# Layer 1's query operands: two transposes per token tile instead of four, the swapped operand copied in SBUF

## The chip, the cores and the metric

The kernel runs on one core of one Trainium2 chip. The metric is the device time of one execution in microseconds (us); lower is better. A core has five engines that run on their own and meet at semaphores: TensorE (PE in the profile, its weight loads PEld), VectorE (DVE), ScalarE (ACT), GpSimd (POOL) and SyncE (SP), which issues the DMAs. Each engine works through its own queue strictly in order. TensorE writes to PSUM, the other engines read PSUM and SBUF.

## The reference

Two layers of a diffusion backbone over 512 latent tokens and 256 context tokens, model width 1024, float32. Layer 0 is a windowed and a dense attention side by side, layer 1 a differential attention; each layer is followed by a SwiGLU network. The change is in layer 1's attention:

```python
q = _rms(q.reshape(b, n, HEADS_C, 2, d), qn)      # 8 heads, 2 halves of 64
k = _rms(k.reshape(b, n, HEADS_C, 2, d), kn)
if use_rope:
    q, k = _rope(q, cos, sin), _rope(k, cos, sin)
...
s = jnp.einsum('bqhad,bkhad->bhaqk', qb, k).astype(jnp.float32) * scale
p = jax.nn.softmax(s, axis=-1)
a = (p[:, :, 0] - lam * p[:, :, 1]).astype(v.dtype)
return jnp.einsum('bhqk,bkhe->bqhe', a, v)
```

Queries come from the 512 latent tokens alone, keys and values from all 768 tokens.

## The kernel before

A float32 product is made of rounded parts. A value v is split into a high part hi (v cast to float32r) and a low part lo = v - hi, and TensorE multiplies the parts. For the scores of layer 1 the parts lie above each other on the partitions: head size is 64, so a stack of two parts fills 128. The key operand `kT[:, a]` holds, for half a, the high part of the keys in partitions 0 to 63 and the low part in 64 to 127. The query operand `qt[:, j, a]` holds one part twice: j = 0 the high part above the high part, j = 1 the low part above the low part. Two matmuls into the same bank (L715 and L716) add up hi·hi + hi·lo and lo·hi + lo·lo.

**Work per head.** Layer 1 has 8 heads, each with six token tiles of 128: two of context (4, 5), then four latent (0 to 3), in the order of `CTX_FIRST`. For each tile `project` sums the input projection in one PSUM bank (`inps`, L465; 24 matmuls, in two halves with other work between). `Proj1.finish` then copies the sums to SBUF on ScalarE (`qkv`, L677), which frees the bank for the next tile; GpSimd copies the values (`vv`, L678); ScalarE squares, VectorE sums the squares (L422) and applies weights and rotation (L427 to L433), GpSimd makes the reciprocal root (`rs_q`, L159, L160) and scales (`qy`, L680). Then the parts are made: `qd` high on ScalarE (L685), `qd` low on VectorE (L686), `kd` high on ScalarE (L688), `kd` low on GpSimd (L689). Some steps later the closure `transposes` turns them on TensorE (`qpt`, L696, four transposes of 128x128 for a latent tile; `kpt`, L702, two) and ScalarE copies the results to SBUF (`qt`, L698; `kT`, L703).

**Attention.** `attend1` handles one tile of 128 queries of one head: eight score matmuls (`sc`, L715, L716, for two halves a), for each half a maximum on VectorE (`mx`, L718) and an exponential on ScalarE (`e`, L720); VectorE combines the halves (`rc`, `rt`, `e`, L723 to L727); TensorE transposes the result (`ppt`, L734), ScalarE and VectorE copy it out (`PT`, L739 and L737), TensorE multiplies with the values (`av`, L744); ScalarE scales (`o`, L746, L749), GpSimd makes a root (`rs_o`), VectorE normalises (`o`, L751).

**How they are woven.** The main loop runs over i, the 32 pairs of head and query tile. One pass issues the scores of i, three steps of the next heads' projection (a step is half a token tile), the transposes and value products of i - 1, and whichever `transposes` closures are due: a closure becomes due five steps after its tile was summed. So a head's projection runs while the head before is attended, and twelve steps make a period of one head. Weights of the next head (`weight1`) are loaded in four units by SyncE, cast on ScalarE (`wih`, L370) and subtracted on GpSimd (`wil`, L371); there are five buffers for them and two for the raw loads.

The order of instructions on each engine is made by the tile framework's scheduler, from dependences and its own estimate of durations. It is fixed at build time, so a change of one instruction can reorder others.

Of the kernel before, what the change touches and what calls it, by code (L numbers as in the profile page):

```python
# [12 lines left out]
F32R = mybir.dt.float32r  # L13
# [6 lines left out]
P = 128  # L20
# [7 lines left out]
HD = 64  # L28
# [23 lines left out]
def bc(ap, pos, n):  # L52

    dims = [list(d) for d in ap.ap]
    return AP(ap.tensor, ap.offset, dims[:pos] + [[0, n]] + dims[pos:])
# [8 lines left out]
def backbone(es: ExitStack, tc: tile.TileContext, x, c, ctx, c_ctx, mod_w, mod_b, norm_mix_w, norm_ffn_w,  # L64
# [3 lines left out]
    nc = tc.nc  # L68
# [33 lines left out]
    def tr_tile(name, shape, dt=F32, one=None):  # L102
        if one is None:
            one = turn["tr"] = 1 - turn["tr"]
        return p_1.tile(shape, dt, name=name, tag=f"tr{one}")
# [10 lines left out]
    def f32(ap):  # L116
        return ap.bitcast(F32)
# [13 lines left out]
    identr = cp.tile([P, P], F32R, name="identr")  # L131
# [248 lines left out]
    def rope_tables(pool, wq, wk):  # L380

        rp = raw_tile([P, NTX, 2, HD], "rp")
        nc.sync.dma_start(rp, rope)
        w = pool.tile([P, 2, HD], F32, name="rw", tag="rw")
        nc.sync.dma_start(w[:, 0, :], dram_rows(wq))
        nc.sync.dma_start(w[:, 1, :], dram_rows(wk))
        nc.vector.tensor_scalar(w[:, 0, :], w[:, 0, :], HD ** -0.5, None, ALU.mult)
        tb = pool.tile([P, 2, NTX, 2, HD], F32, name="rt", tag="rt")
        for j in range(2):
            nc.vector.tensor_tensor(tb[:, j, :, 0, :], rp[:, :, 0, :], bc(w[:, j, :], 1, NTX), ALU.mult)  # L390
            sw = swap_pairs(w[:, j, :])
            nc.vector.tensor_tensor(tb[:, j, :, 1, :].rearrange("p t (a b) -> p t a b", b=2),
                                    rp[:, :, 1, :].rearrange("p t (a b) -> p t a b", b=2),
                                    bc(sw, 1, NTX), ALU.mult)
        return w, tb
# [21 lines left out]
    def rotate_all(raw, h0, n, t, wc, tb, pool):  # L417

        sq = pool.tile([P, n * HD], F32, name="sq", tag="qz", bufs=2)
        nc.scalar.activation(sq, raw, AF.Square)  # L420
        ss = small.tile([P, n], F32, name="qss", tag="qss")
        nc.vector.tensor_reduce(ss, sq.rearrange("p (h d) -> p h d", d=HD), AX.X, ALU.add)  # L422
        r = rsqrt(ss, n, 1.0 / HD, "q")
        y = pool.tile([P, n, HD], F32, name="qy", tag="qy", bufs=2)
        rh = raw.rearrange("p (h d) -> p h d", d=HD)
        if t >= NTX:
            nc.vector.tensor_tensor(y, rh, wc[:, h0:h0 + n], ALU.mult)  # L427
            return y, r
        z = pool.tile([P, n, HD], F32, name="qz", tag="qz", bufs=2)
        nc.vector.tensor_tensor(z.rearrange("p h (a b) -> p (h a) b", b=2),  # L430
                                swap_pairs(raw), tb[:, t, 1].rearrange("p h (a b) -> p (h a) b", b=2), ALU.mult)
        nc.vector.tensor_tensor(y, rh, tb[:, t, 0], ALU.mult)
        nc.vector.tensor_add(y, y, z)  # L433
        return y, r
# [46 lines left out]
    def weights0(b, wp, subs, new_tile=raw_tile, loads=((0, 1), (), (2,), (3,))):  # L481
# [3 lines left out]
        for u in range(4):  # L485
# [13 lines left out]
            subs[u % len(subs)].tensor_sub(lo, raw, f32(hi))  # L499
            yield hi, lo  # L500

    def tables0(j, tabs, wp):
        tabs[j] = rope_tables(wp, *((ev_qn_a[0], ev_kn_a[0]) if j == 0 else (ev_qn_b[0], ev_kn_b[0])))

# [152 lines left out]
    class Proj1:  # L657
# [14 lines left out]
        def finish(self, t, ps):  # L672

            n, wp, kT, qs = self.width(t), self.wp.pool, self.kT, self.qs
            m, h0 = (n - P) // HD, 0 if t < NTX else 2
            raw = wp.tile([P, 384], F32, name="qkv", tag="qkv", bufs=4)
            nc.scalar.copy(raw[:, :n], ps[:, :n])  # L677
            nc.gpsimd.tensor_copy(self.vv[:, t, :], raw[:, n - P:n])  # L678
            y, r = rotate_all(raw[:, :n - P], h0, m, t, self.wc, self.tb, wp)
            nc.gpsimd.tensor_tensor(y, y, bc(r, 2, HD), ALU.mult)  # L680
            nq = m - 2
            if nq:
                qd = wp.tile([P, 2, 2, 2, HD], F32R, name="qd", tag="qd", bufs=3)
                yb = bc(y[:, 0:2], 2, 2)
                nc.scalar.copy(qd[:, 0], yb)  # L685
                nc.vector.tensor_sub(qd[:, 1], yb, f32(qd[:, 0]))  # L686
            kd = wp.tile([P, 2, 2, HD], F32R, name="kd", tag="kd", bufs=3)
            nc.scalar.copy(kd[:, :, 0, :], y[:, nq:nq + 2])  # L688
            nc.gpsimd.tensor_sub(kd[:, :, 1, :], y[:, nq:nq + 2], f32(kd[:, :, 0, :]))  # L689

            def transposes():
                if nq:
                    pt = tr_tile("qpt", [P, 2, 2, P], F32R)
                    for j in range(2):
                        for a in range(2):
                            nc.tensor.transpose(pt[:, j, a, :], qd[:, j, a].rearrange("p a d -> p (a d)"), identr)  # L696
                    qt = self.qp.tile([P, 2, 2, P], F32R, name="qt", tag="qt", bufs=5)
                    nc.scalar.copy(qt, f32(pt))  # L698
                    qs[t] = qt
                pk = tr_tile("kpt", [P, 2, P], F32R)  # L700
                for a in range(2):
                    nc.tensor.transpose(pk[:, a, :], kd[:, a].rearrange("p a d -> p (a d)"), identr)  # L702
                nc.scalar.copy(kT[:, :, t * P:(t + 1) * P], f32(pk))  # L703
            return transposes

    def attend1(h, t, state, o_t, nlam, subln, mp):
        qs, kT, vv = state.qs, state.kT, state.vv
        mx = small.tile([P, 2], F32, name="mx", tag="mx")
        sm = small.tile([P, 2], F32, name="sm", tag="sm")
        E = []  # L710
        for a in range(2):
            sc = p_sc.pool.tile([P, 1024], F32, name="sc", tag="sc", bufs=2)
            for s0, k0, k1 in ((256, SEQ, TOK), (512, 0, SEQ)):
                so = sc[:, s0:s0 + k1 - k0]
                nc.tensor.matmul(so, qs[t][:, 0, a, :], kT[:, a, k0:k1], start=True, stop=False)  # L715
                nc.tensor.matmul(so, qs[t][:, 1, a, :], kT[:, a, k0:k1], start=False, stop=True)  # L716
            s = sc[:, 256:256 + TOK]
            nc.vector.tensor_reduce(mx[:, a:a + 1], s, AX.X, ALU.max, negate=True)  # L718
            e = mp.tile([P, TOK], F32, name="e", tag="e", bufs=PBUF)
            turn["exp"] = nc.scalar.activation(e, s, AF.Exp, bias=mx[:, a:a + 1], accum_out=sm[:, a:a + 1])  # L720
            E.append(e)
        rc = small.tile([P, 2], F32, name="rc", tag="rc")
        nc.vector.reciprocal(rc, sm)  # L723

        rt = small.tile([P, 1], F32, name="rt", tag="rt")
        nc.vector.scalar_tensor_tensor(rt, sm[:, 0:1], nlam, rc[:, 1:2], ALU.mult, ALU.mult)
        nc.vector.scalar_tensor_tensor(E[0], E[1], rt, E[0], ALU.mult, ALU.add)  # L727
        yield
        vt = [4, 5, 0, 1, 2, 3]
        pts = []  # L730
        for g0, m in ((0, 4), (4, 2)):
            pt = tr_tile("ppt", [P, 4, P])
            for a in range(m):
                nc.tensor.transpose(pt[:, a, :], E[0][:, (g0 + a) * P:(g0 + a + 1) * P], ident)  # L734
            PT = mp.tile([P, 4, P], F32, name="PT", tag="PT", bufs=3)
            if g0:
                nc.vector.tensor_copy(PT[:, :m], pt[:, :m])  # L737
            else:
                nc.scalar.copy(PT, pt)  # L739
            pts += [PT[:, a, :] for a in range(m)]  # L740
        yield
        av = acc_tile("av", P, one=1)
        for kc, PT in enumerate(pts):
            nc.tensor.matmul(av, PT, vv[:, vt[kc], :], start=kc == 0, stop=kc == NT - 1)  # L744
        oc = o_t[t][:, h * P:(h + 1) * P]
        nc.scalar.activation(oc, av, AF.Copy, scale=rc[:, 0:1])  # L746
        ss = small.tile([P, 1], F32, name="oss", tag="oss")
        o1 = mp.tile([P, P], F32, name="o1", tag="o1", bufs=2)
        nc.scalar.activation(o1, oc, AF.Square, accum_out=ss)  # L749
        r = rsqrt(ss, 1, 1.0 / P, "o")  # L750
        nc.vector.scalar_tensor_tensor(oc, oc, r, subln, ALU.mult, ALU.mult)  # L751
# [405 lines left out]
    wp = Pool("mw0", "right")  # L1157
# [5 lines left out]
    for t in CTX_FIRST:  # L1163
# [4 lines left out]
        for g in range(2):  # L1168
            pt = tr_tile("npt", [P, 4, P])
# [120 lines left out]
    if True:  # L1290
        for i, (b, t) in enumerate(steps):
            j = i % NT
# [37 lines left out]
            if t == 0:  # L1330
# [13 lines left out]
                wp = Pool("w0", "right")  # L1344
# [219 lines left out]
    wp = Pool("mw1", "right")  # L1564
# [44 lines left out]
    if True:  # L1609
# [40 lines left out]
        def scores(i):  # L1650
            h, t = divmod(i, NTX)
            attend[i] = attend1(h, t, state[h], o_t, nlam, subln, at.pool)
            next(attend[i])
# [73 lines left out]
        wp = Pool("w1", "right")  # L1727
# [203 lines left out]
```

## Time and profile before

| | before |
|---|---|
| time, median of 3 runs | 1695.58 us (1693.07 to 1696.42) |
| span of the profiled execution | 1695.6 us |
| mean granted TensorE clock in it | 0.992 of full speed |

No time is shown for the profiled execution apart from its span; the span equals the median of the runs, so durations read from it can be set against that time directly.

In the rows quoted below, the first number of a timeline row is the start in us from the span's start, the second how long it took, then engine, line, operation, the tiles written and read, shapes and count; in brackets how long the engine had been idle before it and which instruction ended that. Consecutive instructions of an engine overlap a little, so costs are best read from start to next start. A row of busy time by stretches gives, for the stretch in us, its length, then busy time and instructions of PE, PEld, DVE, ACT and POOL, then the granted clock and the DMA engines' share and GB/s. A row of waits gives who waited for whom, us in total, times, longest. A row of a group of instructions ends in its count, busy us in total and mean ns of one, and the idle time before them.

### The profile page before, as it was taken

The page shows a single profiled execution, that of the slowest core. Times are in us where ns is not written, and L with a number is a line of the kernel's source. Part 1 is how long each engine was busy: PE and PEld are TensorE (multiplying, and loading weights), DVE is VectorE, ACT ScalarE, POOL GpSimd, SP SyncE. Part 2 cuts the span into 40 slices and gives each one's busy share as a digit, 9 for nine tenths or more (in the row PEclk, how much of TensorE's full clock was granted, in tenths as well). Part 3 has the DMA queues.
Part 4 walks back from the last instruction along what each step waited for, and adds up shares of the span by engine and source line. Part 5 has one row for each costly group of instructions (what it writes and reads, how often), then busy time and mean ns, then how long its engine had stood idle before and what let it go on. Part 6 is the DMA issues. An engine that isn't in the chain of part 4 may idle for free. (4 is left out here: it accounts for less than half of the span.)

```text
span 1695.6 us, 28585 instructions
## 1 busy us (share of the span) xinstructions
PE 1631.5 (96%) x10390; PEld 1468.6 (87%) x10390; DVE 1146.7 (68%) x2014; ACT 937.0 (55%) x2011; POOL 696.4 (41%) x867
## 2 busy tenths in 40 slices
PE   6999999899999999999999989999999999999998
PEld 3977787677999999998777889999988899999887
DVE  3765656754799887767767656666666598887434
ACT  5565555745456665545554456666666555555320
POOL 2665554321346554412413366666664242221000
PEclk8999999999999999999999999999999999999999
DMA  9222221411455555439966311111112433331431
GB/s 319 69 71 74 70 70 50 164 60 38 129 167 172 164 159 162 134 108 347 296 184 189 99 43 38 48 42 44 50 45 97 125 93 102 111 101 57 137 99 62
DMA packets 218108, 194.64 MB, mean 115 GB/s; under 512 B 20016, under 2 KB 202864, under 8 KB 217968
## 3 DMA queue, kind: packets, MB, share of 16 engines
q1 hardware_dynamic: 217616, 192.62, 36.8%
q8 instruction: 81, 1.33, 0.3%
q14 instruction: 59, 0.48, 0.1%
q10 hardware_dynamic: 352, 0.21, 0.0%
HBM read 179.92 MB, written 12.87 MB: 114 GB/s over the span
## 5 line engine op out<-in xcount | busy, mean ns | idle before, releaser
L901 ACT CAST wbh<-wr 128x512 fp32r<-128x512 f32 x170 | 104.9, 621 | 130.2 <-PE p L933 73.4
L933 PE MATMUL p<-hT,wbh 128*128 128x256 f32 (+1 forms) x752 | 154.5, 299 | 0.0
L465 PE MATMUL inps<-wih,hT 128*128 128x384 f32 x512 | 144.2, 344 | 7.3 <-ACT qkv L677 7.3
L911 POOL TENSOR_TENSOR wbl<-wr,wbh 128x512 fp32r<-128x512 f32 x43 | 60.0, 1396 | 173.6 <-ACT wbh L901 173.6
L933 PEld LDWEIGHTS p<-hT,wbh 128*128 128x128 f32 x752 | 121.9, 191 | 0.2
L911 DVE TENSOR_TENSOR wbl<-wr,wbh 128x512 fp32r<-128x512 f32 x127 | 107.7, 858 | 21.0 <-ACT wbh L901 16.8
L933 PE MATMUL p<-hT,wbl 128*128 128x256 f32 (+1 forms) x376 | 111.9, 298 | 0.0
L933 PE MATMUL p<-t,wbh 128*128 128x384 f32 (+1 forms) x480 | 111.3, 318 | 0.0
L604 POOL TENSOR_SCALAR Pt<-Pt,rc 128x256 f32<-128x256 f32 (+3 forms) x96 | 74.6, 788 | 89.3 <-DVE rc L601 83.1
L231 POOL TENSOR_TENSOR modp<-modp 128x512 f32<-128x512 f32 x40 | 57.4, 1436 | 114.3 <-ACT modp L230 114.3
L465 PEld LDWEIGHTS inps<-wih,hT 128*128 128x128 f32 x512 | 93.3, 188 | 10.6 <-ACT qkv L677 9.7
L933 PE MATMUL p<-hTt,wbh 128*128 128x256 f32 (+1 forms) x480 | 101.0, 302 | 0.0
L887 POOL TENSOR_TENSOR wr<-wr 128x512 f32<-128x512 f32 x40 | 61.6, 1540 | 89.8 <-DVE ws L892 85.8
L933 PE MATMUL p<-b,wbh 128*128 128x384 f32 x368 | 93.8, 336 | 0.2 <-DVE c L961 0.2
L901 ACT CAST wbh<-ws 128x512 fp32r<-128x512 f32 x120 | 69.4, 579 | 43.1 <-PE p L933 29.0
L224 DVE SCALAR_TENSOR_TENSOR ma<-modw,cols,ma 128x256 f32<-128x256 f32 x140 | 89.2, 637 | 2.3
L592 ACT ACTIVATE Pt<-sc,nm 128x256 f32<-128x256 f32 (+3 forms) x96 | 67.6, 707 | 35.3 <-DVE nm L588 16.9
L465 PE MATMUL inps<-wil,hT 128*128 128x384 f32 x256 | 86.0, 336 | 0.0
L933 PEld LDWEIGHTS p<-t,wbh 128*128 128x128 f32 x480 | 82.9, 189 | 0.0
L911 DVE TENSOR_TENSOR wbl<-ws,wbh 128x512 fp32r<-128x512 f32 x120 | 81.7, 681 | 1.7 <-ACT wbh L901 1.6
L933 PEld LDWEIGHTS p<-hTt,wbh 128*128 128x128 f32 x480 | 78.3, 191 | 3.1 <-ACT modp L230 1.6
L230 ACT ACTIVATE modp<-modw,cols 128x256 f32<-128x256 f32 x160 | 68.4, 500 | 18.0 <-POOL ma L236 10.1
(355 smaller groups left out, 5217.9 us busy)
## 6 DMA issues: line engine op xcount, KB each, us to landing
modw<-in_mod_w_dram SPq DMA_DIRECT2D x96, 512.0 KB, 5.2
wr<-in_ffn_w_in_dram SPq DMA_DIRECT2D x176, 256.0 KB, 2.9
wdr<-in_ffn_w_out_dram SPq DMA_DIRECT2D x66, 512.0 KB, 3.7
wir<-in_od_w_in_dram SPq DMA_DIRECT2D x96, 128.0 KB, 2.3
hidm<-hid SPq DMA_DIRECT2D x44, 192.0 KB, 1.9
hr<-hidm SPq DMA_DIRECT2D x22, 192.0 KB, 3.5
x<-in_x_dram SPq DMA_DIRECT2D x8, 512.0 KB, 3.5
wir<-in_ev_w_in_dram SPq DMA_DIRECT2D x16, 256.0 KB, 3.5
```

Source lines behind the costliest of these rows:

```text
L224: nc.vector.scalar_tensor_tensor(acc, w[:, k], scale[k], acc, ALU.mult, ALU.add)
L230: nc.scalar.activation(pr[:, k], w[:, k], AF.Copy, scale=scale[k])
L231: nc.gpsimd.tensor_add(pr[:, 0:2], pr[:, 0:2], pr[:, 2:4])
L465: nc.tensor.matmul(ps, hs[j][:, k, :], ws[k // 2][z][:, k % 2, c0:c1], start=(k, j, z) == (0, 0, 0), stop=(k, j, z) == (KT - 1, 1, 0))
L592: turn["exp"] = nc.scalar.activation(p[:, :n], s, AF.Exp, bias=nm[:, c1], accum_out=sm[:, c1])
L604: nc.gpsimd.tensor_scalar(p[:, :n], p[:, :n], rc[:, hh:hh + 1], 1.0, ALU.mult, ALU.mult)
L887: nc.gpsimd.tensor_sub(w, raw[f, "G1"], w)
L901: nc.scalar.copy(hi, w)
L911: (nc.gpsimd if name == "G2" else nc.vector).tensor_sub(lo, raw[need[n]], f32(hi))
L933: nc.tensor.matmul(ps, w[:, k, :], H[b][h][:, k, :], start=first and k == 0 and q == 0, stop=final and k == 3 and q == 2, skip_group_check ...
```

## The change

The query operand of a latent tile is stored in another way. Before, `qd` holds each part twice and four transposes make both operands. After, `qd` holds high beside low once (as `kd` does), two transposes give the operand high above low, and the second operand, low above high, is copied from the first within SBUF by two VectorE copies that exchange the partition halves. The two matmuls then add up hi·hi + lo·lo and lo·hi + hi·lo: the same four products.

```diff
+    swaps = []
+
+    def swapped(left=0):
+        while len(swaps) > left:
+            to, src = swaps.pop(0)
+            for j in range(2):
+                nc.vector.tensor_copy(to[HD * (1 - j):HD * (2 - j)], f32(src[HD * j:HD * (j + 1)]))
+
+    def halves_swapped(to, src):
+        swaps.append((to, src))
+        swapped(1)
...
-                qd = wp.tile([P, 2, 2, 2, HD], F32R, name="qd", tag="qd", bufs=3)
-                yb = bc(y[:, 0:2], 2, 2)
-                nc.scalar.copy(qd[:, 0], yb)
-                nc.vector.tensor_sub(qd[:, 1], yb, f32(qd[:, 0]))
+                qd = wp.tile([P, 2, 2, HD], F32R, name="qd", tag="qd", bufs=3)
+                nc.scalar.copy(qd[:, :, 0, :], y[:, 0:2])
+                nc.vector.tensor_sub(qd[:, :, 1, :], y[:, 0:2], f32(qd[:, :, 0, :]))
...
-                    pt = tr_tile("qpt", [P, 2, 2, P], F32R)
-                    for j in range(2):
-                        for a in range(2):
-                            nc.tensor.transpose(pt[:, j, a, :], qd[:, j, a].rearrange("p a d -> p (a d)"), identr)
+                    pt = tr_tile("qpt", [P, 2, P], F32R)
+                    for a in range(2):
+                        nc.tensor.transpose(pt[:, a, :], qd[:, a].rearrange("p a d -> p (a d)"), identr)
                     qt = self.qp.tile([P, 2, 2, P], F32R, name="qt", tag="qt", bufs=5)
-                    nc.scalar.copy(qt, f32(pt))
+                    nc.scalar.copy(qt[:, 0], f32(pt))
+                    halves_swapped(qt[:, 1], qt[:, 0])
...
     def attend1(h, t, state, o_t, nlam, subln, mp):
...
+        swapped()
         for a in range(2):
```

The copies of a tile are issued when the next tile is turned, and at the latest ahead of the next scores. The order on TensorE, but for the groups of two instead of four, and on SyncE stays as it was. On ScalarE, VectorE and GpSimd the scheduler places some other instructions differently too. The rows below are one head's period in layer 1 in the middle of the loop; a row is line, operation, output<-inputs and shape, and lines behind 510 are 10 to 12 higher after the change.

ScalarE before, around the first two attention tiles of a period (`wih` is a weight cast, `e` an exponential):

```order
L370 CAST wih<-wir 128x768
L720 ACTIVATE e,sm<-sc,mx 128x768
L685 CAST qd<-qy 128x256
L688 CAST kd<-qy 128x2x64
L370 CAST wih<-wir 128x768
L739 COPY PT<-ppt 128x512
L720 ACTIVATE e,sm<-sc,mx 128x768
L677 COPY qkv<-inps 128x256
```

The same place after the change:

```order
L370 CAST wih<-wir 128x768
L696 CAST qd<-qy 128x2x64
L699 CAST kd<-qy 128x2x64
L370 CAST wih<-wir 128x768
L732 ACTIVATE e,sm<-sc,mx 128x768
L751 COPY PT<-ppt 128x512
L732 ACTIVATE e,sm<-sc,mx 128x768
L689 COPY qkv<-inps 128x256
```

The first exponential moved from ahead of `qd`, `kd` and the second weight cast to behind them.

ScalarE before, some ten instructions later, at the next attention tile's exponentials:

```order
L685 CAST qd<-qy 128x256
L688 CAST kd<-qy 128x2x64
L720 ACTIVATE e,sm<-sc,mx 128x768
L677 COPY qkv<-inps 128x256
L688 CAST kd<-qy 128x2x64
L720 ACTIVATE e,sm<-sc,mx 128x768
L420 ACTIVATE sq<-qkv 128x128
L739 COPY PT<-ppt 128x512
```

The same place after the change:

```order
L696 CAST qd<-qy 128x2x64
L699 CAST kd<-qy 128x2x64
L732 ACTIVATE e,sm<-sc,mx 128x768 x2
L689 COPY qkv<-inps 128x256
L699 CAST kd<-qy 128x2x64
L751 COPY PT<-ppt 128x512
L420 ACTIVATE sq<-qkv 128x128
```

Both exponentials now stand ahead of the copy `qkv`; `PT` moved ahead of the square.

VectorE after the change, from the start of the period on (`CAST qt` are the new copies, two per tile):

```order
L433 TENSOR_TENSOR qy<-qy,qz 128x256
L508 CAST qt<-qt 64x256 x2
L432 TENSOR_TENSOR qy<-qkv,rt 128x256
L430 TENSOR_TENSOR qz<-qkv,rt 128x256
L508 CAST qt<-qt 64x256 x2
L730 TENSOR_REDUCE mx<-sc 128x1
L433 TENSOR_TENSOR qy<-qy,qz 128x256
L422 TENSOR_REDUCE qss<-sq 128x4
L730 TENSOR_REDUCE mx<-sc 128x1
L697 TENSOR_TENSOR qd<-qy,qd 128x2x64
```

Two pairs of copies came in ahead of the period's first maximum; before the change the rows are the same without them, save that `qd` stood behind the normalisation of `o`. Two more pairs come in later in the period, one ahead of the second attention tile's maxima, which then run directly one after the other with `qd` behind both.

## The prediction

> **What bounds the kernel now.** I read the page's first part, then busy time by stretches, then the waits of TensorE, then every instruction of one head of layer 1 in order of time.
>
> ```profile
> span 1695.6 us, 28585 instructions
> PE 1631.5 (96%) x10390; PEld 1468.6 (87%) x10390; DVE 1146.7 (68%) x2014; ACT 937.0 (55%) x2011; POOL 696.4 (41%) x867
> 980.00:1000.00 20.00, 15.65 (x112) 14.35 (x111) 10.21 (x19) 11.31 (x30) 16.33 (x28) 1.00 0.26 72
> 1056.70:1096.41 39.71, 39.02 (x278) 37.62 (x277) 25.76 (x53) 26.09 (x68) 26.29 (x42) 1.00 0.14 41
> PE inps L465 <- ACT qkv L677: 4.1, 6, 1.3
> PEld inps L465 <- POOL wil L371: 2.6, 6, 1.2
> ```
>
> TensorE (PE) is busy 96% of the span. The changed code runs from about 985 to 1275 us: a start (head 0, PE busy 15.65 of 20 us), six like periods of some 39.7 us, one per head, and a tail. In a period PE works 39.02 of 39.71 us at full clock (1.00), so what PE no longer executes looks like pure gain. But the last two rows say that six times each, once a period, PE still waits: for ScalarE's copy of the finished sums (`qkv`, which frees the only bank) and for GpSimd's weight residual (`wil`). Where such a wait ends last, PE time saved ahead of it is worth nothing. So I price by place, in the period that starts at 1056.70.
>
> **Transposes removed.** Two of four go, per latent token tile: 32 tiles, 64 transposes.
>
> ```profile
> 1068.51 0.54 PE L696 MATMUL qpt<-identr,qd 128*128 128x128 f32 x4
> 1068.88 0.34 PE L702 MATMUL kpt<-identr,kd 128*128 128x128 f32 x2
> 1087.81 0.37 PE L702 MATMUL kpt<-identr,kd 128*128 128x128 f32 x2
> 1088.02 0.40 PE L465 MATMUL inps<-wih,hT 128*128 128x384 f32 x1
> ```
>
> Behind the same kind of product, four take 0.37 us from start to next start (1068.51 to 1068.88), two take 0.21 (1087.81 to 1088.02): 0.16 saved per tile, 0.65 per period of four tiles, 32 x 0.16 = 5.1 us in all if every bit counted.
>
> It doesn't. Two of the four tiles are turned at the period's start, ahead of this wait:
>
> ```profile
> 1056.70 0.83 ACT L370 CAST wih<-wir 128x768 fp32r<-128x768 f32 x1 [0.60 <-PE inps L465]
> 1057.62 1.95 POOL L371 TENSOR_TENSOR wil<-wir,wih 128x768 fp32r<-128x768 f32 x1 [1.94 <-ACT wih L370]
> 1064.68 1.84 POOL L371 TENSOR_TENSOR wil<-wir,wih 128x768 fp32r<-128x768 f32 x1
> 1066.58 0.19 PEld L465 LDWEIGHTS inps<-wil,hTc 128*128 128x128 f32 x1 [0.28 <-POOL wil L371]
> ```
>
> PE frees a weight buffer, ScalarE casts at 1056.70, GpSimd works from 1057.62 without a gap to 1066.52, and PE waits 0.28 for that. An earlier PE only waits longer: 0.32 of the 0.65 is lost. The other two tiles, turned later, count: **-0.32 per period**.
>
> A small gain stands at the period's end. Before the wait there, VectorE ran the wide `qd` subtraction between two maxima, and the second maximum leads to the exponential and then to `qkv`:
>
> ```profile
> 1069.34 0.28 DVE L427 TENSOR_TENSOR qy<-qkv,rc 128x128 f32<-128x128 f32 x1
> 1092.34 0.41 DVE L686 TENSOR_TENSOR qd<-qy,qd 128x256 fp32r<-128x256 f32 x1
> 1092.68 0.94 DVE L718 TENSOR_REDUCE mx<-sc 128x1 f32<-128x768 f32 x1
> 1095.07 0.44 PE L465 MATMUL inps<-wih,hT 128*128 128x384 f32 x1 [0.61 <-ACT qkv L677]
> ```
>
> At half width it should cost what the 128-column row does, 0.28 for 0.41: **-0.13 per period**. The shorter casts on ScalarE (26.09 busy of 39.71) shorten no wait that I found.
>
> **Order on ScalarE, second attention tile.** The change moves the second exponential ahead of `qkv`.
>
> ```profile
> 1072.44 0.90 ACT L720 ACTIVATE e<-sc,mx 128x768 f32<-128x768 f32 x1
> 1073.24 0.19 ACT L720 ACTIVATION_READ_ACCUMULATOR e<-sc,mx 128x1 f32 x1
> 1073.55 0.37 ACT L677 COPY qkv<-inps 128x256 f32<-128x256 f32 x1
> 1074.36 0.90 ACT L720 ACTIVATE e<-sc,mx 128x768 f32<-128x768 f32 x1
> 1072.32 0.41 DVE L686 TENSOR_TENSOR qd<-qy,qd 128x256 fp32r<-128x256 f32 x1
> 1072.65 0.95 DVE L718 TENSOR_REDUCE mx<-sc 128x1 f32<-128x768 f32 x1
> 1073.36 0.82 PE L734 MATMUL ppt<-cst,e 128*128 128x128 f32 x6
> 1073.98 0.44 PE L465 MATMUL inps<-wih,hT 128*128 128x384 f32 x1
> ```
>
> Now `qkv` runs 1073.55 to 1073.92 and PE starts the next sums at 1073.98, with no loss. After the change both maxima run back to back, the second from 1072.32 to 1073.26; the second exponential starts when ScalarE is done with the first, 1072.44 + 0.90 = 1073.34, its accumulator read from 1074.14, and `qkv` 0.10 later: 1074.24 to 1074.61. PE starts some 0.05 behind it, at 1074.66, against 1073.98: **+0.68 per period**. Queued behind `qkv` are only the `kd` cast, `PT` and a square, all with room. That the same queue order costs is seen at 1095.07: there two exponentials already stand ahead of `qkv`, and PE waits 0.61. Bounds: 0 (if PE were late anyway) and 0.9 (a whole exponential).
>
> **Order on ScalarE, first attention tile.** The first exponential moves behind a weight cast that needs a DMA.
>
> ```profile
> 1063.94 0.90 ACT L720 ACTIVATE e<-sc,mx 128x768 f32<-128x768 f32 x1
> 1065.33 0.83 ACT L370 CAST wih<-wir 128x768 fp32r<-128x768 f32 x1
> 1066.06 0.58 ACT L739 COPY PT<-ppt 128x512 f32<-128x512 f32 x1
> 1067.25 1.50 PE L744 MATMUL av<-vv,PT 128*128 128x128 f32 x12
> 1106.36 0.83 ACT L370 CAST wih<-wir 128x768 fp32r<-128x768 f32 x1 [1.23 <-DMA wir<-in_od_w_in_dram]
> 1107.73 1.60 PE L744 MATMUL av<-vv,PT 128*128 128x128 f32 x12 [0.58 <-ACT PT L739]
> ```
>
> `PT` starts 0.73 behind the cast (1065.33 to 1066.06); with the exponential between them, 0.73 + 0.90. The cast can come up to 0.8 earlier, since the exponential is gone from in front of it, if its data are there: `PT` then ends between 1066.7 and 1067.5, against PE's need at 1067.25: 0 to 0.3, I take 0.1. Where the DMA is late, as at 1106.36, the whole 0.9 falls on PE, which waits for `PT` already. Five periods have this order, one with the late DMA: 4 x 0.1 + 0.9 = **+1.3 in all** (bounds 0 and 5 x 0.9 = 4.5).
>
> **The copies.** Per tile two VectorE copies of 64x256, SBUF to SBUF; no row shows that shape.
>
> ```profile
> L407 DVE COPY rw<-rw 128x64 f32<-128x64 f32 x2 | 0.4, 190 | 0.0
> L411 DVE COPY rc<-rw 128x128 f32<-128x128 f32 x2 | 0.4, 219 | 0.0
> L737 DVE COPY PT<-ppt 128x256 f32<-128x256 f32 x32 | 13.4, 418 | 6.7 <-PE ppt L734 6.6
> ```
>
> From 64 to 128 columns costs 0.029 us, so 256 columns are 0.219 + 2 x 0.029 = 0.28; bounds 0.219 and 0.418 (a source in PSUM). VectorE has 39.71 - 25.76 = 14 us idle a period, against 8 x 0.28 = 2.2. No scores wait for them: a head's four query tiles are turned during the attention of the head before. Their price is what they do to GpSimd:
>
> ```profile
> 1067.77 1.64 DVE L726 SCALAR_TENSOR_TENSOR rt<-sm,nlam,rc 128x1 f32<-128x1 f32 x1
> 1067.56 1.83 POOL L371 TENSOR_TENSOR wil<-wir,wih 128x768 fp32r<-128x768 f32 x1
> ```
>
> A one-column VectorE instruction ends at 1069.41, just behind GpSimd's subtraction (1069.39): one engine waits for the other's whole instruction. Four copies a period stand in GpSimd's gapless stretch ahead of 1066.52, on which PE waits. Each may push it by its length or fit into a gap: 0 to 4 x 0.28 = 1.1 per period. I take one copy's length, **+0.3 per period**, nearer the low end since some of GpSimd's instructions there are short.
>
> [...]
>
> **Start and tail.** At the start PE waits for GpSimd (16.33 of 20 us busy), so saved transposes count little there and copies may cost: 0, bounds -0.6 and +1. In the tail the last `qd` moves behind the long `e`:
>
> ```profile
> 1269.09 0.43 DVE L686 TENSOR_TENSOR qd<-qy,qd 128x256 fp32r<-128x256 f32 x1 [0.20 <-ACT qd L685]
> 1269.43 1.22 DVE L727 SCALAR_TENSOR_TENSOR e<-e,rt 128x768 f32<-128x768 f32 x1
> 1269.79 0.75 PE L696 MATMUL qpt<-identr,qd 128*128 128x128 f32 x4 [0.76 <-ACT qt L698]
> ```
>
> `e` takes `qd`'s place, so `qd` ends at about 1270.3 to 1270.6 and PE's transposes, now at 1269.79, start 0.5 to 0.8 later, less 2 x 0.16 for the shorter groups: **+0.3** (0 to 0.5). The four copies behind it run while PE is in `av`.
>
> **The sum.** Six periods x (-0.32 - 0.13 + 0.68 + 0.3) = +3.2; the DMA cast +1.3; tail +0.3: **+4.8 us**. The profiled span, 1695.6, equals the median of the three times, 1695.58, so 1695.6 + 4.8 = **1700.4 us**.
>
> **Rivals.**
> - *Pure PE gain*: the new order on ScalarE does no harm (qkv is ready as before) and GpSimd's stretch shrinks with the rest, so all 28 tiles behind the start save: 28 x 0.16 = 4.5 us, 1691.1. For it: PE busy 98% of a period. Against: the two waits that end last each period. It holds if the second exponential costs PE under 0.1 a period. Faster.
> - *A draw*: the transposes' gain and the second exponential are as priced, but the copies fit into gaps and the DMA cast is always early: 6 x 0.23 + 0.3 = +1.7, 1697.3. Within 0.2%.
> - *Port*: all four copies displace GpSimd's stretch, 1.1 for 0.3 a period: +4.8 more, 1705.2.
> - *Not what it says*: the program's order shows two transposes fewer per tile and the same PE order besides, so I give it nothing.
>
> **Chances.** Forecast (1699 to 1703) 0.43, port 0.14, draw 0.25, pure gain 0.18. 0.2% is 3.4 us, about what a measurement of this kernel can tell from no change. So faster 0.18, same 0.26, slower 0.56. The range leaves out the faster half of the gain case and the far end of the port case: 1691.5 to 1706.
>
> **What would show it.** In a period after: `kpt` behind `qpt` 0.21 instead of 0.37 (transposes); the wait for `wil` 0.5 or more instead of 0.28 (lost saving; above 0.8, port); a new wait of about 0.7 of `inps` for `qkv` where 1073.98 is now; 0.5 instead of 0.61 at 1095.07; period 40.2 instead of 39.7. A period under 39.4 with no new wait for `qkv` would prove me wrong, as would copies far from 0.28, or scores that wait for VectorE.

## The result

The changed kernel takes 1702.59 us (median of 6 runs, 1698.76 to 1707.53) against 1695.07 us before (6 runs, 1693.07 to 1696.42) on the same chip: ratio 1.0047, 95% interval 1.0031 to 1.0063. Run again on another chip, beside 23 runs of before, it took 1701.66 us, ratio 1.0038 (1.0023 to 1.0053). It is 6 to 8 us slower; the forecast was 1700.4, and 4.8 slower.

The profiled execution of the changed kernel is its fastest run (1698.76); 1.76 us of it lie outside the span, and the other runs have about as much, so before's profiled execution was one of about 1697.4 us. So the two profiles are compared place by place, not by their spans: the part ahead of layer 1's first `kpt` alone is 3.5 us shorter in the profile after (976.28 for 979.79 us), and between profiles of the changed kernel and of e7 below, whose programs are the same up to there, it differs by 3.0 (976.28 and 979.24). The first lines of the page after the change:

```profile
span 1697.0 us, 28524 instructions
PE 1626.2 (96%) x10326; PEld 1461.5 (86%) x10326; DVE 1156.5 (68%) x2078; ACT 927.1 (55%) x2011; POOL 698.0 (41%) x867
```

Two stretches of it, the start and one period (length, busy time of PE, PEld, DVE, ACT, POOL, then granted clock, DMA share, GB/s):

```profile
980.00:1000.00 20.00, 15.57 (x109) 14.45 (x110) 12.81 (x28) 10.17 (x30) 16.10 (x28) 1.00 0.15 41
1053.39:1094.33 40.94, 38.83 (x270) 37.09 (x269) 26.01 (x61) 24.83 (x68) 26.46 (x42) 1.00 0.14 40
```

And TensorE's waits from 1020 to 1262 us (us in total, times, longest):

```profile
PE inps L465 <- ACT qkv L689: 5.6, 12, 1.2
PE av L756 <- ACT PT L751: 3.2, 4, 1.2
PE inps L465 <- POOL wil L371: 2.8, 6, 0.6
```

TensorE executes 64 transposes fewer and is busy 5.3 us less, yet the end comes later: what it saved, and more, went into waits. It now waits for `qkv` twice a period (12 times) instead of once, and for `PT` four times.

The signs that the prediction named, in the period from 1053.39 on (at 40.94 us a little longer than the mean of 40.69 below, as the 39.71 of before is a little shorter than its 40.01). First TensorE and its weight loads: the transposes, the wait for `wil`, the new wait for `qkv` (the load's and the product's), the wait at the period's end.

```profile
1066.38 0.37 PE L706 MATMUL qpt<-identr,qd 128*128 128x128 f32 x2
1066.59 0.33 PE L713 MATMUL kpt<-identr,kd 128*128 128x128 f32 x2
...
1063.28 0.19 PEld L465 LDWEIGHTS inps<-wil,hTc 128*128 128x128 f32 x1 [0.63 <-POOL wil L371]
1072.34 0.19 PEld L465 LDWEIGHTS inps<-wih,hT 128*128 128x128 f32 x1 [0.69 <-ACT qkv L689]
1072.34 0.44 PE L465 MATMUL inps<-wih,hT 128*128 128x384 f32 x1 [0.45 <-ACT qkv L689]
1092.97 0.45 PE L465 MATMUL inps<-wih,hT 128*128 128x384 f32 x1 [0.34 <-ACT qkv L689]
```

`kpt` stands 0.21 behind `qpt`; the wait for `wil` is 0.63 instead of 0.28, so the saving of two tiles (0.32) went into it; the wait of 0.69 for `qkv` is there; the one at the end is 0.34 instead of 0.61. Then ScalarE: the second attention tile's exponentials with `qkv` behind both, and the first attention tile, with TensorE's `av` that waits for `PT`.

```profile
1071.04 0.89 ACT L732 ACTIVATE e<-sc,mx 128x768 f32<-128x768 f32 x1
1071.92 0.37 ACT L689 COPY qkv<-inps 128x256 f32<-128x256 f32 x1
...
1062.77 0.83 ACT L370 CAST wih<-wir 128x768 fp32r<-128x768 f32 x1 [1.33 <-DMA wir<-in_od_w_in_dram]
1063.51 0.90 ACT L732 ACTIVATE e<-sc,mx 128x768 f32<-128x768 f32 x1
1064.39 0.57 ACT L751 COPY PT<-ppt 128x512 f32<-128x512 f32 x1
1065.02 1.61 PE L756 MATMUL av<-vv,PT 128*128 128x128 f32 x12 [0.89 <-ACT PT L751]
```

Here the prediction was too mild. It let the DMA be late in one period of five. The cast waits in all five, by 0.50, 1.33, 0.65, 1.28 and 1.63 us; the exponential stands behind it, `PT` behind the exponential, and TensorE behind `PT`. TensorE's products wait in four of the five, by 0.89, 0.23, 0.86 and 1.19 us (3.2 in all).

To compare kernels by place I take TensorE's first `av` product of each head: five periods lie between the first head's and the sixth's.

| TensorE, us | before | after | after, again |
|---|---|---|---|
| start: first `kpt` to first `av` | 38.05 | 37.84 | 38.02 |
| five periods | 200.03 | 203.45 | 203.39 |
| one period | 40.01 | 40.69 | 40.68 |
| sixth period | 40.90 | 40.85 | 40.95 |
| tail, to the last `av` | 52.27 | 54.03 | 54.06 |
| sum | 331.25 | 336.17 | 336.42 |

In the profiles the change costs 4.9 to 5.2 us, 3.4 of it in the five periods (0.68 each) and 1.8 in the tail.

### The profile page after: what moved, and what is told of

The parts are those of the page before. It is cut to its first block, busy times and chain, and to the rows that moved or that the text cites. A ratio compares the mean times of both kernels' runs of the same rounds, so it can differ in the third digit from the quotient of the medians.

```text
span 1697.0 us, 28524 instructions
## 1 busy us (share of the span) xinstructions
PE 1626.2 (96%) x10326; PEld 1461.5 (86%) x10326; DVE 1156.5 (68%) x2078; ACT 927.1 (55%) x2011; POOL 698.0 (41%) x867
## 3 DMA queue, kind: packets, MB, share of 16 engines
q8 instruction: 81, 1.33, 0.3%
```

## The experiments

The question: is it ScalarE's new order that costs, or the copies? The first four kernels take the two new orders and the copies apart. The orders are put back by an edge in the scheduler's graph that holds no data (`exps` lists the exponentials; `queue_behind(a, b)` puts `a` behind `b` on one engine).

```diff
 # second attention tile: the second exponential behind qkv (e1, e3)
-            nc.scalar.copy(raw[:, :n], ps[:, :n])
+            turn["qkv"] = nc.scalar.copy(raw[:, :n], ps[:, :n])
+            if t == CTX_FIRST[1] and len(exps) > 1 and (len(exps) // 2 - 1) % NTX == 3:
+                queue_behind(exps[-1], turn["qkv"])
 # first attention tile: the weight cast behind the first exponential (e1, e2)
-            new_head([weight1(h, u, wh, nc.gpsimd) for u in range(4)])
+            with tc.issue_after(exps[-10].ins) if len(exps) >= 10 else ExitStack():
+                u0 = weight1(h, 0, wh, nc.gpsimd)
+            new_head([u0] + [weight1(h, u, wh, nc.gpsimd) for u in range(1, 4)])
 # no copies (e4)
-                    halves_swapped(qt[:, 1], qt[:, 0])
...
-                nc.tensor.matmul(so, qs[t][:, 1, a, :], kT[:, a, k0:k1], start=False, stop=True)
+                nc.tensor.matmul(so, qs[t][:, 0, a, :], kT[:, a, k0:k1], start=False, stop=True)
```

Both orders back (e1):

> Both new orders on ScalarE are undone, everything else of the change is kept: the first exponential of a head stands ahead of the weight casts that wait for DMA again, and the second exponential of the second tile stands behind the copy qkv again. If the orders are what costs (theory), the period falls to about 39.2 (39.8 of before, less 0.3 for the transposes and 0.3 for the shorter wait at its end) and the time to 1691 to 1693, below before's 1695.1. [...]

The first tile's order back (e2):

> Only the first tile's order is undone (the first exponential ahead of the casts that wait for DMA); the second exponential still stands ahead of qkv. Theory: the waits of av for PT (0.2 to 1.2 us a period) go, the waits of 0.45 to 0.7 us of inps for qkv stay; 3 to 5 us faster than the changed kernel: 1697 to 1700. Rival (copies): 1702 to 1703, no change.

The second tile's order back (e3):

> Only the second tile's order is undone (second exponential behind qkv); the first exponential still stands behind the casts. Theory: the six waits of 0.45 to 0.7 us of inps for qkv go, the waits of av for PT stay: 3 to 4 us faster than the changed kernel, 1698.5 to 1700. Rival (copies): 1702 to 1703, no change.

No copies (e4):

> The copies of the halves are left out: the second product of the scores reads the same operand as the first, so it computes high times high plus low times low twice over. The order of ScalarE is then that of the second kernel of this set: the first exponential ahead of the casts, the second one ahead of qkv. So the price of the copies is the difference to that kernel. Theory (copies hidden): within 1 us of it, 1696.5 to 1700. Rival (copies cost by GpSimd's waits, 0.3 to 1.1 a period): 2 to 7 us below it.

Measured, with the ratio to before (1694.05 us, 30 runs) and the lengths of the same places:

| kernel | median us | ratio, 95% | one period | tail |
|---|---|---|---|---|
| e1 both back | 1695.33 | 1.0005 (0.9992 to 1.0017) | 39.58 | 54.96 |
| e2 first back | 1697.34 | 1.0022 (1.0010 to 1.0033) | 40.06 | 53.89 |
| e3 second back | 1698.81 | 1.0031 (1.0020 to 1.0041) | 39.96 | 54.48 |
| e4 no copies | 1695.65 | 1.0014 (1.0003 to 1.0024) | 39.91 | 53.65 |

The orders are the loss: alone, each gives back 0.63 (e2) or 0.73 us (e3) of a period; together 1.11, and the ratio is that of no change. ScalarE in e1, at the two places:

```profile
1064.41 0.90 ACT L741 ACTIVATE e<-sc,mx 128x768 f32<-128x768 f32 x1
1065.21 0.19 ACT L741 ACTIVATION_READ_ACCUMULATOR e<-sc,mx 128x1 f32 x1
1065.82 0.83 ACT L370 CAST wih<-wir 128x768 fp32r<-128x768 f32 x1 [0.42 <-DMA wir<-in_od_w_in_dram]
...
1073.44 0.37 ACT L689 COPY qkv<-inps 128x256 f32<-128x256 f32 x1
1073.71 0.91 ACT L741 ACTIVATE e<-sc,mx 128x768 f32<-128x768 f32 x1
```

The cast still waits for its DMA, but nothing that TensorE needs at once stands behind it. The periods of e1 are 0.43 us shorter than before's, as the prediction's two gains say (0.32 + 0.13); but 1691 to 1693 was expected and 1695.3 came, because the start (39.25 for 38.05) and the tail (54.96 for 52.27) took the gain. Those two are taken up below.

e4 is compared with e2, which has the copies and the first exponential ahead of the late cast as well (in e4 it stands ahead of `qd` and `kd` too): 0.16 us a period, and 1695.65 against 1697.34 with intervals that overlap; that lies between e4's two forecasts. It is also no more than two kernels with the same order in the periods differ by (39.58 in e1, 39.41 in e8 below). So the copies by themselves cost little; how much, these profiles can't tell. But without them the scheduler leaves the first exponential where it was (the second one moves all the same): the copies' larger price is the order that they brought about. In after and in e4, the first cast of a period, GpSimd's second subtraction, and (of after) the third one, (of e4) the fourth cast; after's fourth is the 1062.77 above:

```profile
1053.39 0.83 ACT L370 CAST wih<-wir 128x768 fp32r<-128x768 f32 x1 [0.60 <-PE inps L465]
1056.85 1.88 POOL L371 TENSOR_TENSOR wil<-wir,wih 128x768 fp32r<-128x768 f32 x1
1061.39 1.83 POOL L371 TENSOR_TENSOR wil<-wir,wih 128x768 fp32r<-128x768 f32 x1
```

```profile
1052.66 0.83 ACT L370 CAST wih<-wir 128x768 fp32r<-128x768 f32 x1 [0.59 <-PE inps L465]
1055.99 1.85 POOL L371 TENSOR_TENSOR wil<-wir,wih 128x768 fp32r<-128x768 f32 x1
1061.19 0.83 ACT L370 CAST wih<-wir 128x768 fp32r<-128x768 f32 x1
```

From the period's first cast the subtraction ends after 5.34 us with the copies (1056.85 + 1.88 - 1053.39) and after 5.18 without; the fourth cast starts after 9.38 and 8.53, the first with a wait of 1.33 for the DMA, the second with none. The load for that cast waits for the subtraction, which frees its buffer: SyncE issues it 5.41 and 5.24 us behind the first cast.

So the copies make the load some 0.16 us later. They don't explain the 0.85 between 9.38 and 8.53: in the five periods of after, the load is issued 5.3 to 5.4 us behind the first cast each time, yet the fourth cast starts after 8.56, 9.38, 8.71, 9.33 and 9.68 us. The transfers themselves take different times, the median part 2.2 us to landing in the first and third period and 3.4 in the fifth; why stays open.

Next, the orders without the rest of the change (e5), the copies doubled (e6), TensorE kept busy in the tail (e7), and the tail's order put back as well (e8):

```diff
 # e5: before, with the new orders (exponential behind cast, qkv behind second exponential)
+                if u == 0 and len(exps) >= 10:
+                    queue_behind(exps[-10], turn["cast"])
...
+                queue_behind(turn["qkv"], exps[-1])
 # e6: after, with every copy twice
-            for j in range(2):
+            for j in (0, 1, 0, 1):
 # e7: after, with ten products more ahead of the tail's first output sum
+                for _ in range(10 if k == 0 else 0):
+                    nc.tensor.matmul(part.ps, tile_T(0, 0)[:, 0, :], oproj.ws[0][0][:, :512], start=True, stop=True)
 # e8: e1, and in the tail the copies behind hT, the long e behind qd
+            with behind("low"):
+                for j in range(2):
...
-        swapped()
+        if (h, t) != (6, 2):
+            swapped()
...
+        if (h, t) == (6, 2):
+            queue_behind(mix, turn["qd"])
```

> The kernel before, with its four transposes and no copies, but with ScalarE in the order of the changed kernel: the first exponential behind the casts that wait for DMA, the second one ahead of qkv. Theory (the orders cost 1.1 us a period, by the first three kernels): periods of 41.1 instead of 40.0 us, 1699 to 1702. If the loss needs the copies or the shorter transposes as well: 1694 to 1696, no change.

> The changed kernel with each copy of the halves made twice over; the order of ScalarE is that of the changed kernel. Theory (copies lie beside other work in the periods): periods within 0.2 us of the changed kernel's 40.7, and some 0.3 to 0.6 us more in the tail, 1702 to 1704. Rival (a copy costs 0.07 to 0.28 us by GpSimd's waits or VectorE's queue): 1704 to 1709.

> The changed kernel with ten more copies of the first product of the output projection in the tail, just ahead of TensorE's wait of 2.5 us for hT (each starts the sum anew, so the result stays). If the granted clock of 0.50 over 6.8 us of the tail follows from this idle time and costs 1.7 us more than before's 3.3 us at 0.50: the clock stays at 1.00 for one or both windows, and the time falls to 1699 to 1701. If VectorE's chain alone sets the tail: 1702 to 1704.

> Both orders of ScalarE undone as in the first kernel, and the order of VectorE in the tail put back too: the last qd ahead of the long e, and the copies behind hT there. Theory: the wait of ops for hT falls from 2.7 to about 1.9 us and that of qpt for qd from 1.7 to under 0.8; with periods of 39.6 the time is 1691 to 1694, below before's 1694. If the tail is set by the halved clock and by hT alone: 1694.5 to 1696, as the first kernel.

| kernel | median us | ratio, 95% (before 1694.13, 23 runs) | one period | tail |
|---|---|---|---|---|
| e5 before, new orders | 1704.64 | 1.0055 (1.0042 to 1.0067) | 41.51 | 53.43 |
| e6 copies twice | 1713.94 | 1.0120 (1.0104 to 1.0136) | 42.96 | 54.21 |
| e7 tail filled | 1700.51 | 1.0041 (1.0028 to 1.0053) | 40.74 | 53.82 |
| e8 orders and tail back | 1692.07 | 0.9988 (0.9977 to 1.0000) | 39.41 | 53.23 |

e5 shows the orders from the other side: on the old transposes, without a copy, they cost 1.5 us a period and 9.3 us in all by the ratio, more than forecast (1699 to 1702). But ScalarE's order in e5 isn't quite that of the changed kernel: the cast `kd` came to stand between the second tile's two exponentials, and in three periods of five it waits there for GpSimd. TensorE's waits in e5 from 1015 to 1255 us, and that cast:

```profile
PE inps L465 <- ACT qkv L677: 8.8, 11, 1.3
PE av L754 <- ACT PT L749: 1.3, 2, 1.0
1073.85 0.30 ACT L690 CAST kd<-qy 128x128 fp32r<-128x128 f32 x1 [0.54 <-POOL qy L682]
```

In the same stretch the changed kernel waits 4.4 us for `qkv` and 3.2 for `PT`. So e5 shows that the second tile's order costs without any copy, and makes it dearer than it is in the changed kernel. The first tile's order makes TensorE wait 1.3 us in e5, less than half of the 3.2: there too the cast waits for its DMA in four of five periods (0.48, 0.44, 1.51 and 0.83 us), but two of these loads come soon enough for `PT`, and in the period without that wait TensorE waits for `wil` first (0.5 us).

e6 was a miss, for both theories: 12 us more than the changed kernel by the ratios (1.0120 and 1.0047), and it lies in the periods (42.96 for 40.69), whose order on ScalarE and GpSimd is the changed kernel's. GpSimd, VectorE and TensorE of e6 in order of time, in one period:

```profile
1022.87 2.06 POOL L371 TENSOR_TENSOR wil<-wir,wih 128x768 fp32r<-128x768 f32 x1
1023.60 1.48 DVE L508 CAST qt<-qt 64x256 fp32r<-64x256 f32 x1
1025.76 1.81 POOL L371 TENSOR_TENSOR wil<-wir,wih 128x768 fp32r<-128x768 f32 x1
1026.10 1.61 DVE L508 CAST qt<-qt 64x256 fp32r<-64x256 f32 x1
1028.68 0.71 PE L756 MATMUL av<-vv,PT 128*128 128x128 f32 x4 [1.91 <-DVE PT L749]
```

And a wait of TensorE that is new, from 1015 to 1255 us:

```profile
PE av L756 <- DVE PT L749: 8.5, 6, 2.0
```

A copy that takes 0.29 us in the changed kernel took 1.48 and 1.61 where it came up inside GpSimd's subtraction, and ended with it (1023.60 + 1.48 = 1025.08; 1022.87 + 2.06 = 1024.93). Maxima and `PT` stand behind it. In the changed kernel the pairs fall between the subtractions and take 0.59, as here:

```profile
1056.43 0.59 DVE L508 CAST qt<-qt 64x256 fp32r<-64x256 f32 x2 [1.76 <-ACT qt L708]
```

So the copies are nearly free only where they stand; the next ones were not. The waiting of one engine for the other's instruction that the prediction priced is there, but it mostly holds up VectorE, not GpSimd: from 1020 to 1255 us a copy takes 0.55 us in the mean in e6 and 0.29 in the changed kernel, a subtraction 1.95 and 1.89. In the two rows above the subtraction had started first, by 0.73 and 0.34 us.

e8 came out as forecast (1691 to 1694): the waits in the tail (1255 to 1315 us) after the change and in e8 are

```profile
PE ops L821 <- DVE hT L812: 2.5, 1, 2.5
PE qpt L706 <- DVE qd L697: 1.2, 1, 1.2
```

```profile
PE ops L835 <- DVE hT L826: 1.9, 1, 1.9
PE qpt L709 <- DVE qd L700: 0.8, 1, 0.8
```

It is the only kernel below before, by 2 us of 1694, with an interval that touches no change. Its wait for `wil` (3.4 us between 1015 and 1255) was then the largest, beside that for `qkv` (3.3). Two last kernels tried to take it, beside a repeat of the changed kernel (in the first table):

```diff
 # e10: e8, the second unit's subtraction on VectorE; e11: the third's
-            new_head([u0] + [weight1(h, u, wh, nc.gpsimd) for u in range(1, 4)])
+            new_head([u0] + [weight1(h, u, wh, nc.vector if u == 1 else nc.gpsimd) for u in range(1, 4)])
```

> The changed kernel as it is, once more. [...]

> The kernel with both orders and the tail put back, and in addition the subtraction wil of the second of a head's four weight units on VectorE instead of GpSimd. If the wait of inps for wil (0.5 us a period) is what keeps half of the transposes' saving back: it falls under 0.1, periods fall from 39.4 to 38.9 to 39.1 and the time to 1689 to 1691.5. If VectorE has no room beside the copies: the waits of av for PT or inps for qkv grow by as much, 1692 to 1695.

> As the kernel before, with the third weight unit's subtraction on VectorE instead of the second's; it is the one that inps waits for, and it falls beside the maxima of the scores. If the wait for wil counts: below 0.1 as well, 1689 to 1692; if VectorE's queue around the maxima counts more: the exponentials come some 0.9 us later and the time is 1693 to 1697.

e9: periods of 40.68, as in the first profile of the changed kernel (40.69); median 1701.66. e10: 1698.65 us, ratio 1.0024 (1.0014 to 1.0033), periods 40.54; e11: 1696.84, ratio 1.0013 (1.0001 to 1.0025), periods 40.13. Both are slower than e8; e10 lies above both of its forecasts, e11 in the range of its second, with waits for `wil` of 2.2 us still there. In e10 the waits for `wil` are gone, but 7.3 us of waits for VectorE's `PT` came in their place (1015 to 1255 us):

```profile
PE av L770 <- DVE PT L763: 7.3, 6, 1.5
```

VectorE and GpSimd of e10 in one period:

```profile
1054.34 0.94 DVE L371 TENSOR_TENSOR wil<-wir,wih 128x768 fp32r<-128x768 f32 x1
1056.18 2.22 DVE L509 CAST qt<-qt 64x256 fp32r<-64x256 f32 x2 [0.89 <-ACT qt L711]
1056.41 1.84 POOL L371 TENSOR_TENSOR wil<-wir,wih 128x768 fp32r<-128x768 f32 x1
```

The moved subtraction took 0.94 us of VectorE; GpSimd's next one now falls on a pair of copies, which takes 2.22 instead of 0.59.

## Why the prediction came out right

- **Transposes and what the wait for `wil` keeps back**: as forecast, 0.16 a tile, and half of it lost (the weight load's wait 0.63 for 0.28).
- **Period's end**: right in kind, too small: the wait fell by 0.27, not 0.13.
- **Second attention tile, +0.68 a period**: right. The new wait is 0.69 on the weight load, and taking it back gave 0.73 a period (e3).
- **First attention tile, +1.3 in all**: the mechanism was right, the term mis-sized: taking it back gave 0.63 a period (e2), 3.1 us in five. The step that failed is "one with the late DMA". TensorE waits 0.86 to 1.19 us for `PT` in three of the five periods and 0.23 or less in the other two: the cast, without the exponential ahead of it, could have come up to 0.8 us earlier, but its load has not landed, and it starts 8.56 to 9.68 us behind the period's first cast (8.63 in the period of before that was priced, with the exponential ahead of it). In e5, without copies, the same waits come to 1.3 us. But whether the copies make three loads late instead of one is not shown, since the transfers differ among themselves by more than the copies' 0.16.
- **Copies**: duration right (0.29 for 0.28). No run shows the +0.3 a period for GpSimd work that the copies displace, and it was put on the wrong wait: the third subtraction ends 9.83 us behind the first cast (1061.39 + 1.83 - 1053.39), before 9.82 (1064.68 + 1.84 - 1056.70). By e2 and e4 they cost about 0.16 a period in all, which is as much as the same order differs by from e1 to e8.
- **Start 0**: right (37.84 and 38.02 for 38.05). **Tail +0.3**: too small, 1.8. The last `qd` went behind the long `e` as said; that the copies ahead of the maxima delay `hT` too (wait 2.5 for 1.4) was not seen, and a longer stretch at half clock came beside it (3.4 us of clock lost for 1.7, below).
- **Sum**: 4.8 forecast, 4.9 and 5.2 in the profiles, by errors of both signs: by the parts of the table the sum had 5 x 0.53 + 1.3 = +3.95 in the five periods (measured 3.4), +0.53 in the sixth (measured -0.05 and +0.05) and +0.3 in the tail (measured 1.8). The copies' price at GpSimd was too dear, the late load and the tail too cheap. So the mechanisms on ScalarE were right, and that the parts add up so near to 4.8 is luck. The six periods of before were not alike either, as the prediction took them ("some 39.7"): they ran from 39.70 to 40.90. The ratios say 8.0 (5.3 to 10.7) and 6.4 (3.9 to 9.0); what they show beyond the profiles stays open. That the span of before equalled the median was chance: its execution was 2.3 us above the median, so the step from 1695.6 to 1700.4 added a difference to a span where a time belonged.

## What to carry to other kernels

Read what a change does to the order of in-order queues before pricing what it removes: here 64 transposes saved less than two exponentials cost that changed places on ScalarE, and the scheduler moved one of them only because of the new copies. An instruction that others wait for should not stand behind one that waits for a DMA, even if that DMA is on time today: here TensorE came to wait 3.2 us for `PT` behind such a cast, for 0.7 before. Idle time on an engine was not room everywhere: eight copies a period fitted into VectorE's 14 us at 0.29 us each; with eight more, copies came up inside GpSimd's subtractions and took 1.48 and 1.61 us, and the whole cost some 12 us.

## What the runs showed of the hardware

The granted clock of TensorE fell to 0.50 for 3.4 us in the start of e1 and in the tail of before, and for 6.8 us in the tail of after (in steps of 1 us 0.81, 3 x 0.50 and 0.99 from 1269 us on, and 0.62, 6 x 0.50 and 0.97 from 1268 us on: 1.70 and 3.41 us of clock lost). e1's start, in the same steps:

```profile
993.00:994.00 1.00, 0.57 (x7) 0.39 (x5) 0.29 (x1) 0.83 (x4) 1.00 (x2) 1.00 0.03 9
994.00:995.00 1.00, 0.24 (x2) 0.10 (x2) 0.59 (x3) 0.61 (x2) 1.00 (x3) 1.00 0.00 0
995.00:996.00 1.00, 0.66 (x4) 0.66 (x5) 0.73 (x2) 0.25 (x1) 1.00 (x3) 0.93 0.00 0
996.00:997.00 1.00, 1.00 (x4) 1.00 (x4) 0.41 (x1) 0.62 (x3) 0.84 (x4) 0.50 0.00 0
...
999.00:1000.00 1.00, 1.00 (x9) 0.90 (x8) 0.00 (x0) 0.40 (x2) 0.16 (x1) 0.86 0.00 0
```

The clock lost there is 0.07 + 3 x 0.50 + 0.14 = 1.71 us: 3.4 us at half speed. The order of ScalarE, VectorE and GpSimd up to there is that of the changed kernel, whose two profiles have no such stretch; e3, e7, e8 and e10 have it (1.70 to 1.71 us of clock lost in each). What it costs is seen from the `kpt` behind TensorE's last wait of 1.1 us there to the first product that waits for `kT`: 6.2 us in the changed kernel's two profiles, 7.3 to 7.4 with the stretch. So 1.71 us of lost clock are 1.2 us of time. The tail of before, of after, of e5 and of e7 (1262 to 1310 us):

```profile
1262.00:1310.00 48.00, 43.84 (x270) 37.37 (x269) 33.09 (x59) 33.88 (x76) 23.77 (x38) 0.96 0.30 95
```

```profile
1262.00:1310.00 48.00, 42.20 (x255) 35.86 (x254) 34.75 (x65) 32.39 (x75) 23.46 (x36) 0.93 0.27 91
```

```profile
1262.00:1310.00 48.00, 43.23 (x268) 37.80 (x269) 34.05 (x61) 33.36 (x80) 26.66 (x42) 0.93 0.27 88
```

```profile
1262.00:1310.00 48.00, 43.89 (x275) 38.15 (x274) 35.73 (x68) 31.31 (x77) 27.10 (x42) 0.96 0.29 89
```

Before loses 0.04 x 48 = 1.9 us of clock (1.70 by the steps), after 0.07 x 48 = 3.4, about twice; but e5, which has before's order in the tail and the same waits (1.4 us for `hT`), loses 3.4 as well. So whether one stretch follows or two is not set by the change alone. In the three us from 993 on, at whose end the clock fell in e1, TensorE was busy for 0.57, 0.24 and 0.66; in the changed kernel it was busy for 0.59, 0.34 and 0.54 of the three from 990 on, and the clock stayed at 1.00. So what sets off a stretch, and what sets its length, is not shown.

e7 was meant to test whether the idle time in the tail brings the half clock: its ten products filled most of the wait for `hT` (0.4 us are left), one stretch followed behind the wait for `qd` (1.7 us) all the same, and the tail was 0.2 us shorter than that of after. The median (1700.51 for 1701.66 and 1702.59) lies in the range that was forecast for the clock, but shows no difference beyond the intervals.

Two tails show the clock and the order apart, in the tail's 1.8 us. e5 has before's order but two stretches, and lasts 1.2 us longer than before's (53.43 for 52.27). e7 has the order of after and one stretch, as before, and lasts 1.6 us longer (53.82), with the ten products in it. Each alone gives most of the 1.8, so they overlap, and how they share it stays open. Single profiles of the same code differ by a stretch or not, 1.2 us of time, which is as much as the change's own terms.
